# Out-projection of a flow-matching step: seven products of quarters for eight, the gate in W_out, sums joined from PSUM

## The chip, the cores and the metric

The kernel runs on one core of a Trainium2 chip. Its time is in device microseconds, the median of several runs. TensorE (PE; its weight loads are shown as PEld), VectorE (DVE), ScalarE (ACT) and GpSimd (POOL) compute; SyncE (SP) and GpSimd also issue transfers. Each engine has its own instruction queue and takes it in order; semaphores join the queues.

## The reference

One layer for two groups of tokens, 2048 sample tokens and 128 prompt tokens, model width 1024. Cut to what the change touches (the mixer's three branches, all ahead of `merged`, stay as they are):

```python
gt = jax.nn.sigmoid(gates.reshape(B, T, N_BRANCH, D_MODEL))
merged = jnp.einsum('btnd,btnd->btd', gt, pb)
out = jnp.einsum('btd,de->bte', merged, w_out)     # 1024 x 1024, the same for both groups
h = h + gate[:, None, :] * out                     # gate: one row of 1024 for each group
y = rmsnorm(h, final_g)
```

## The kernel before

A Python function records the instructions of each engine; a scheduler with its own timeline then sets their order, within data dependences and priorities (`tc.high_priority`). `order` rows below are that result. Tokens stand in 17 tiles of 128 (0 to 15 sample, 16 prompt). A float32 operand is scaled by a power of two and split into a high and a low f16 part, and a product is three f16 matmuls for each 128 of the contraction: high x high, high x low, low x high. The scale comes from a sum of squares (`A.activation(..., AF.Square, accum_out=...)`), summed over the partitions by a matmul with ones (`scales`: tiles named `...scb` go in, one column comes out).

`xh` and `xl` hold the normalized input in f16 for the whole kernel. `merge(n, ...)` runs once for each branch (order 1, 2, 0): over 8 blocks `db` of 128 model columns, over two halves of the tokens, over token blocks of 512 (one of 128): a gate product of 24 matmuls (`xh`, `xl`), a sigmoid on ACT into `sg`, a branch product of 12 (`big`, that is `o16`), a multiplication on DVE out of PSUM, an addition on POOL into `mrow`, which goes to the DRAM tensor `mD` (`mrg`). The products take their PSUM bank from `ps_mm`, a pool of three. In the last merge (n = 0) `each` is `tail`: `out_w(db)` loads one 128-column block of W_out and splits it into `whi`, `wlo` (`wohi`, `wolo` in rows), and `gate_rows` (the generator `gates`) forms the gate rows in DRAM (`gateD`). At its last block `ahead_out` prepares the first five out tiles (`out_prep`: load from `mD`, square, scale, split into `mh`, `ml`).

The out-projection then goes tile by tile, prompt tile first, then sample tiles 8 to 15 and 0 to 7: two halves of 512 columns with 24 matmuls each (`gemm_N`), on DVE a multiplication of PSUM by `gt` (the gate row times the scales' inverses, made by POOL), on POOL the addition of the x rows `xr`, on ACT the square of the row, `rsqrt` on DVE and POOL, a scaling by `final_g` on DVE, and the store. The last tile has its end split in two halves.

Of the kernel before, what the change touches and what calls it, by code (L numbers as in the profile page):

```python
# [20 lines left out]
P = 128  # L21
# [90 lines left out]
def hybrid_flow_kernel(ctx: ExitStack, tc: tile.TileContext, x_prompt, x_sample, state_delta, c, c_ctx, ln_g, w_ada,  # L112
# [65 lines left out]
    def scales(ss, pl, tag, sb16=None):  # L178

        ps = bank(ps_x, [P, 1])  # L180
        mm(ps, ones16, widened(ss, pl, tag) if sb16 is None else sb16)
        t = sb(pl, [P, 4], tag)
        V.tensor_copy(t[:, 0:1], ps)
        h = t[:, 3:4].bitcast(I32)
        V.tensor_scalar(h, t[:, 0:1].bitcast(I32), 24, None, ALU.logical_shift_right)
        V.tensor_scalar(t[:, 1:2].bitcast(I32), h, -8388608.0, 204.0 * 8388608, ALU.mult, ALU.add)
# [1175 lines left out]
    def merge(n, first, inv, each=None, halves=HALVES, mid=None, then=None):  # L1362

        steps, sinv = iter(()), None
        for db in range(KT):
# [8 lines left out]
            for h0, hn, tbs in halves:  # L1374
                mrow = sb(big, [P, hn], "mrow", bufs=2)
                if not first:
                    SY.dma_start(mrow, mD[db][:, h0:h0 + hn])
                if each is not None and (n == 0 or db > 3):
                    next(gates, 0)
                for t0, tn in tbs:  # L1380
                    if first and db == 0:
# [18 lines left out]
                    pace.tick(tn * MT)  # L1400
                    if sinv is not None:
# [40 lines left out]


    orp = pool(ctx, "orp", 1, side="right")
    whi = sb(orp, [P, KT, D], "wohi", F16)
    wlo = sb(orp, [P, KT, D], "wolo", F16)
    winv = sb(orp, [P, KT], "winv8")

    def out_w(i):
        w = load_w(w_out[0][:, i * P:(i + 1) * P], KT, hi=whi[:, :, i * P:(i + 1) * P], lo=wlo[:, :, i * P:(i + 1) * P])  # L1450
        V.tensor_mul(winv[:, i:i + 1], w.inv, sx)

    def out_prep(t, pl, tag, hl=None):
        mt = sb(pl, [P, KT, P], tag, bufs=2)
        SY.dma_start(mt, mD[:, :, t * P:(t + 1) * P].rearrange("k p t -> p k t"))
        if hl is None:
            mh = sb(orp, [P, KT, P], "mh", F16, bufs=3)
            ml = sb(orp, [P, KT, P], "ml", F16, bufs=3)
        else:
            mh = sb(wp, [P, KT, P], "whi", F16, bufs=4)  # L1460
            ml = sb(wp, [P, KT, P], "wlo", F16, bufs=4)
        ss = sb(orp, [P, 1], "mss", bufs=2)
        with tc.high_priority():
            A.activation(ml, mt, AF.Square, accum_out=ss)
            s, inv = scales(ss, orp, "msc")
            A.activation(mh, mt, AF.Copy, scale=s)  # L1466
            V.scalar_tensor_tensor(ml, mt, s, mh, ALU.mult, ALU.subtract)
        inv8 = sb(orp, [P, KT], "inv8", bufs=6)
        V.tensor_scalar(inv8, winv, inv, None, ALU.mult)
        return mh, ml, inv8  # L1470

    pre, gp = [], []

    def half_gate(i):
        t = sb(ep, [P, 512], "st", bufs=3)
        SY.dma_start(t, gateD[1:2, i * 512:(i + 1) * 512].to_broadcast([P, 512]))
        gp.append(t)

    def ahead_out(h0):
        if h0:  # L1480
            for i, t in enumerate(order[:5]):
                pre.append(out_prep(t, *((wp, "wst") if i % 3 else (big, "mrow")), None if i < 3 else wp))
            for i in range(2):
                half_gate(i)
                scale_gate(gp[i], gp[i], pre[0][2][:, 4 * i:4 * i + 4])

    def scale_gate(out, src, inv):
        k = inv.shape[-1]
        G.tensor_tensor(out.rearrange("p (k x) -> p k x", k=k), src.rearrange("p (k x) -> p k x", k=k),
                        inv.rearrange("p (k o) -> p k o", o=1).to_broadcast([P, k, P]), ALU.mult)  # L1490

    order = [16] + list(range(8, 16)) + list(range(8))
    def tail(db):
        out_w(db)
        if db == KT - 1:
            for _ in gates:
                pass

    merge(0, False, inv_, tail, HALVES[::-1], ahead_out)
    ms_.close()  # L1500
    wo = _W()
    wo.hi, wo.lo = whi, wlo
    op = pool(ctx, "op", 2)
    gb = sb(op, [P, D], "gb", bufs=1)
    SY.dma_start(gb, gateD[0:1, :].to_broadcast([P, D]))
    fg = sb(op, [P, D], "fg", bufs=1)
    SY.dma_start(fg, final_g[None, :].to_broadcast([P, D]))

    part = sb(op, [P, 2], "part", bufs=1)
    for i_, t in enumerate(order):  # L1510
        mh, ml, inv8 = pre[i_]
        xr = sb(op, [P, D], "xr")
        SY.dma_start(xr, xrows(t * P, P))
        hh = sb(op, [P, D], "hh")
        if i_:
            gt = sb(op, [P, D], "gt")
            scale_gate(gt, gb, inv8)
        for i in range(2):
            cs = slice(i * 512, (i + 1) * 512)
            ps = bank(ps_mm, [P, 512])  # L1520
            gemm_N(ps, mh, ml, wo, i * 512, 512)
            dst, gc = (hh[:, cs], gt[:, cs]) if i_ else (gp[i], gp[i])
            with tc.high_priority():
                V.tensor_tensor(dst, ps, gc, ALU.mult)
            (V if i_ == 16 else G).tensor_tensor(hh[:, cs], dst, xr[:, cs], ALU.add)
            if i_ == 16:
                A.activation(xr[:, cs], hh[:, cs], AF.Square, accum_out=part[:, i:i + 1])
        if i_ < 12:
            pre.append(out_prep(order[i_ + 5], op, "mt"))
        ss2 = sb(op, [P, 1], "hss")  # L1530
        if i_ == 16:
            G.tensor_tensor(ss2, part[:, 0:1], part[:, 1:2], ALU.add)
        else:
            A.activation(xr, hh, AF.Square, accum_out=ss2)
        rsqrt(ss2, ss2, 1.0 / D, 1)
        for cs in ([slice(0, 512), slice(512, D)] if i_ == 16 else [slice(0, D)]):
            V.scalar_tensor_tensor(hh[:, cs], hh[:, cs], ss2, fg[:, cs], ALU.mult, ALU.mult)
            SY.dma_start(y_sample[0, t * P:(t + 1) * P, cs] if t < 16 else y_prompt[0, :, cs], hh[:, cs])


_INS = ['x_prompt', 'x_sample', 'state_delta', 'c', 'c_ctx', 'ln_g', 'w_ada', 'b_ada', 'w_in', 'conv_w', 'a_log',
# [24 lines left out]
```

## Time and profile before

| | us |
|---|---|
| median of 3 runs (2187.1 to 2194.83) | 2187.12 |
| profiled execution | 2189.41 |
| its span, first to last instruction | 2187.6 |
| last merge, about | 1735 to 2001 |
| out-projection, first to last matmul | 2002.71 to 2179.8 |
| from there to the end of the span | 7.8 |

Of the page, the first lines give the busy time of each engine; a row of a group reads: line, engine, operation, output and inputs by name, shapes, count, then busy time, mean duration of one in ns, and the idle time of the engine just before, with what ended it. A matmul's own duration (379 ns at 512 columns) holds its pipeline; what it costs in a row of matmuls is the distance of two starts. The mean granted TensorE clock of the execution is 0.991.

### The profile page before, as it was taken

What the parts mean: (1) busy time and instruction counts of PE and PEld (TensorE: products, weight loads), DVE (VectorE), ACT (ScalarE), POOL (GpSimd) and SP (SyncE); (2) the same over time, 40 slices, a digit from 0 to 9 for tenths busy, and PEclk for the clock granted to TensorE, in tenths of its full rate; (3) what the DMA queues carried; (4) which work ended last, traced back from release to release, by engine and by line L of the source; (5) the groups of instructions that cost most, each with busy time, mean ns of one, the idle gap of its engine ahead of it and who ended that gap; (6) DMA issues with size and microseconds to landing.
All of it is one profiled execution on the core that took longest, in us unless ns stands there. A gap on an engine that the chain in (4) does not pass through costs nothing.

```text
span 2187.6 us, 42676 instructions
## 1 busy us (share of the span) xinstructions
PE 2123.6 (97%) x16234; PEld 1214.9 (56%) x16234; DVE 1320.9 (60%) x3150; ACT 1015.0 (46%) x2355; POOL 701.6 (32%) x862
## 2 busy tenths in 40 slices
PE   7999999999999998999899999999999999999998
PEld 3565444455555587878555556555554444444443
DVE  5746854469879698776665555765663544323454
ACT  3644744345566474554544445655543422222332
POOL 1421333223334324322312223344432221222543
PEclk9999999999999999999999999999999999999999
DMA  8424823167777664544655555766654544324542
GB/s 282 141 87 148 290 95 106 61 204 222 253 232 240 198 197 139 146 121 127 197 183 157 174 160 180 242 196 203 198 173 150 174 129 129 116 78 127 173 148 103
DMA packets 304727, 365.09 MB, mean 167 GB/s; under 512 B 39585, under 2 KB 215946, under 8 KB 302474
## 3 DMA queue, kind: packets, MB, share of 16 engines
q1 hardware_dynamic: 289386, 302.19, 45.4%
q0 software_dynamic: 12688, 51.27, 6.5%
q10 hardware_dynamic: 2448, 8.91, 1.0%
q8 instruction: 127, 2.08, 0.4%
q14 instruction: 78, 0.64, 0.1%
HBM read 234.67 MB, written 127.62 MB: 166 GB/s over the span
## 4 chain that ended last, share of the span: by engine, by line
PE 50%; DMA 4%; DVE 4%; ACT 1%; issue 1%; POOL 0%; SPq 0%; DVEq 0%; POOLq 0%; ACTq 0%
PE b L161 50%; DMA st<-br 1%; DMA ES<-ei 1%; DMA mrg<-mrow 1%; DMA wst<-in_w_in_dram 0%; DVE XB L797 0%; DVE E L798 0%; DVE big L1360 0%; DMA mrow<-mrg 0%; DMA S<-in_state_delta_dram 0%; DMA wst<-in_w_branch_dram 0%; PE b L1057 0%; ACT big L1359 0%; DMA sq__2210_18514<-qT 0%; DMA qk<-n 0%
## 5 line engine op out<-in xcount | busy, mean ns | idle before, releaser
L161 PE MATMUL b<-xh,whi 128*128 128x512 f16 (+1 forms) x1920 | 652.6, 349 | 1.4 <-DVE mrow L1395 1.0
L161 PE MATMUL b<-xl,whi 128*128 128x512 f16 (+1 forms) x1920 | 652.9, 349 | 0.0
L161 PE MATMUL b<-xh,wlo 128*128 128x512 f16 (+1 forms) x1920 | 651.6, 348 | 0.0
L161 PEld LDWEIGHTS <-whi 128*128 128x128 f16 x3904 | 358.1, 98 | 329.2 <-issue 10.2
L161 PEld LDWEIGHTS <-wlo 128*128 128x128 f16 x1952 | 191.6, 98 | 179.0 <-issue 3.6
L161 PE MATMUL b<-big,bhi 128*128 128x512 f16 (+1 forms) x960 | 249.7, 347 | 1.4 <-ACT big L1359 1.1
L1399 POOL TENSOR_TENSOR mrow<-mrow,sg 128x512 f32<-128x512 f32 (+1 forms) x80 | 92.6, 1158 | 282.9 <-DVE sg L1398 220.5
L161 PE MATMUL b<-big,blo 128*128 128x512 f16 (+1 forms) x480 | 163.1, 347 | 0.0
L1389 ACT ACTIVATE sg<-b,winv 128x512 f32<-128x512 f32 (+1 forms) x120 | 74.2, 618 | 172.0 <-PE b L161 171.1
L161 PEld LDWEIGHTS <-xh 128*128 128x128 f16 x1496 | 117.7, 98 | 28.0
L161 PEld LDWEIGHTS <-bhi 128*128 128x128 f16 x960 | 86.9, 98 | 75.6
L1398 DVE SCALAR_TENSOR_TENSOR sg<-b,binv,sg 128x512 f32<-128x512 f32 (+1 forms) x80 | 53.4, 667 | 121.4 <-PE b L161 118.7
L646 POOL TENSOR_TENSOR cy<-cy,raw 128x545 f32<-128x545 f32 (+1 forms) x48 | 66.4, 1408 | 185.7 <-ACT raw L645 185.7
L175 DVE CAST wscb<-wss 128x1 bf16<-128x1 f32 x93 | 14.3, 154 | 154.5 <-ACT wlo L209 71.4
L866 POOL COPY T<-ES 32x256 f16<-32x256 f16 x68 | 31.0, 456 | 220.1 <-DMA ES<-ei 217.6
L161 PE MATMUL b<-whi,xh 128*128 128x128 f16 x544 | 94.0, 220 | 0.0
L161 PE MATMUL b<-wlo,xh 128*128 128x128 f16 x544 | 93.9, 220 | 0.0
L161 PE MATMUL b<-whi,xl 128*128 128x128 f16 x544 | 93.8, 220 | 0.0
L161 PE MATMUL b<-wohi,mh 128*128 128x512 f16 x240 | 90.9, 379 | 1.3 <-ACT mh L1466 1.3
L161 PE MATMUL b<-wohi,ml 128*128 128x512 f16 x240 | 90.8, 379 | 0.3 <-DVE mscb L175 0.3
L161 PE MATMUL b<-wolo,mh 128*128 128x512 f16 x240 | 90.9, 379 | 0.0
L209 ACT ACTIVATE wlo<-wst 128x1024 f16<-128x1024 f32 x52 | 54.9, 1056 | 77.4 <-DMA wst<-in_w_in_dram 75.5
(456 smaller groups left out, 4298.1 us busy)
## 6 DMA issues: line engine op xcount, KB each, us to landing
wst<-in_w_in_dram SPq DMA_DIRECT2D x60, 512.0 KB
qkv<-cy POOLq DMA_DIRECT2D x12, 1089.0 KB, 5.2
st<-br SPq DMA_DIRECT2D x48, 256.0 KB
mrow<-mrg SPq DMA_DIRECT2D x18, 512.0 KB
mrow<-mrg SPq DMA_DIRECT2D x16, 576.0 KB
mrg<-mrow POOLq DMA_DIRECT2D x16, 576.0 KB, 3.6
dc<-dec SPq DMA_DIRECT2D x17, 512.0 KB
kq<-qkv SPq DMA_DIRECT2D x34, 256.0 KB
```

What stands on the lines that cost most here:

```text
L161: PE.matmul(out, l, r, start=start, stop=stop)
L175: V.tensor_copy(sb16, ss)
L209: A.activation(w.lo, st, AF.Square, accum_out=ss)
L646: G.tensor_tensor(y[:, c0:c1], y[:, c0:c1], raw[:, 1 + c0:1 + c1], ALU.mult)
L866: G.tensor_copy(T16[rows(a0, b), :, :, b], ES[0:32, :, 2 * a0 + b, :, wT])
L1389: A.activation(sg, ps, AF.Sigmoid, scale=gw.inv)
L1398: V.scalar_tensor_tensor(sg, ps, binv[:, 1:2], sg, ALU.mult, ALU.mult)
L1399: G.tensor_tensor(mr, mr, sg, ALU.add)
```

## The change

Sample tiles are taken in eight pairs. With a pair's rows as A (tile a above tile b), split at the middle of the contraction into four quarters, and W_out likewise, the four quarters of the result are built from seven products (Winograd's form) in place of eight. Of A the sums are `a21 + a22`, that minus `a11`, `a11 - a21`, and `a12` minus the second (`pair_sums`, four POOL additions); the seven operands are then split into f16 (`pair_operands`) and stand in the memory of `xl`, two pairs at a time. Of W four operands stay in `gq` and three are stored to DRAM (`tw`) and read back into the memory of `xh` when the last merge is over. The sample gate row is multiplied into W_out beforehand, so one scale for all of W_out and one for a pair (`minv`) remain, and a result is joined to the x rows in one DVE operation out of PSUM (`joined`); sums of products pass through `sg` tiles and POOL (`added`). The prompt tile comes last, with W_out without the gate, split by 128-column block as before, stored to DRAM (`uw`) and read back; its 192 matmuls have 128 columns each.

`out_weights` does the work on W_out in the last merge, one step after each token block: eight loads with a square, split, store, multiplication by the gate row and second square (`squared`, `ungated`), then eight loads again that form the quarters (`quarters`). Operations in `kept` keep their program order. `formed` takes its bank by `rot[0]`: `bank(ps_d, ...)` raises that counter once more itself, so that its parity stays.

SP's queue at the end of the last merge, before (`mrow ... 128x8x128`, `wst ... 128x8x128`, `mt` are merged rows for out tiles; `mrow ... 128x1024` belongs to the merge):

```order
L1377 DMA mrow_25225<-mrg 128x1152 [waits DMAHW5_49,DMASW3_49,Pool_49]
L1455 DMA mrow_25354<-mrg 128x8x128 [waits DMASW5_49,DMAHW6_49,DMASW4_49,Pool_49]
L1455 DMA wst_25373<-mrg 128x8x128 [waits DMAHW3_49,DVE_49]
L1455 DMA wst_25392<-mrg 128x8x128 [waits DMAHW4_49,DVE_49]
L1455 DMA mrow_25411<-mrg 128x8x128 [waits DMAHW7_49,Pool_49]
L1377 DMA mrow_25455<-mrg 128x1024 [waits DMAHW0_49,DVE_49]
L1455 DMA wst_25430<-mrg 128x8x128 [waits DMAHW1_49,DVE_49]
L1505 DMA gb_25547<-gate 128x1024 [waits DMASW6_49,DMAHW3_49,DVE_49,DMAHW4_49,PE_49,Pool_49]
```

SP's queue there, after (`xh<-tw` are the three stored quarters, `uw` prompt weights, `hh` x rows):

```order
L1377 DMA mrow_25616<-mrg 128x1024 [waits DMAHW2_49,DMASW4_49,Pool_49]
L1540 DMA wst_25590<-mrg 128x8x128 [waits DMAHW3_49,DMASW5_49]
L1540 DMA wst_25592<-mrg 128x8x128 [waits DMAHW4_49]
L1599 DMA xh_93<-tw 128x4096 [waits DMAHW6_49,DMAHW5_49,PE_49]
L1599 DMA xh_93<-tw 128x4096 [waits PE_49]
L1599 DMA xh_93<-tw 128x4096 [waits DMAHW7_49,DMAHW1_49,PE_49]
L1699 DMA whi_26852<-uw 128x1024 [waits DMAHW0_49,PE_49]
L1699 DMA wlo_26853<-uw 128x1024 [waits PE_49]
L1540 DMA mt_25719<-mrg 128x8x128 [waits DMASW6_49,DMAHW2_49,PE_49,Pool_49]
L1540 DMA mt_25721<-mrg 128x8x128 [waits DMAHW3_49]
L1605 DMA hh_25725<-in_x_sample_dram 128x1024 [waits DMAHW4_49]
L1605 DMA hh_25727<-in_x_sample_dram 128x1024 [waits DMAHW5_49]
```

Two loads of merged rows come first instead of five tiles' worth, and the second pair's (`mt`) stand behind the quarters and some prompt weights, with the x rows of the first pair behind them.

TensorE's queue at the first out matmul, before:

```order
L161 MATMUL b_25526<-big_13808,blo_25145 128x512
L161 LDWEIGHTS ones_2_89
L161 MATMUL b_25379<-mscb_25380,ones_2_89 128x1 [waits DVE_49]
L161 LDWEIGHTS mh_25356 [waits Activation_49]
L161 MATMUL b_25555<-wohi_23213,mh_25356 128x512
```

TensorE's queue between the fourth and the fifth product of the first pair, after:

```order
L161 MATMUL b_25824<-xh_93,xl_94 128x512
L161 LDWEIGHTS ones_2_89
L161 MATMUL b_25748<-mscb_25749,ones_2_89 128x1 [waits DVE_49]
L161 LDWEIGHTS xl_94 [waits DMAHW5_49]
L161 MATMUL b_25806<-xh_93,xl_94 128x512 [waits DVE_49]
```

The scale matmul of the next tile stood ahead of the first out product; that of the second pair now stands ahead of the first pair's fifth product, whose bank (`b_25806`) is the first product's.

ACT's queue in the middle of the last merge, before:

```order
L1389 ACTIVATE sg_24429<-b_24404,winv_24213 128x512 [waits PE_49,Pool_49]
L209 ACTIVATE wolo_23214,wss_24661<-wst_24659 128x8x128 [waits DMAHW5_49,Activation_49]
L209 ACTIVATE wlo_24722,wss_24723<-wst_24640 128x1024 [waits DMAHW3_49,Activation_49]
L1389 ACTIVATE sg_24475<-b_24450,winv_24213 128x512 [waits PE_49,Pool_49]
L222 ACTIVATE wohi_23213<-wst_24659,wsc_24667 128x8x128 [waits DVE_49]
```

And after:

```order
L1389 ACTIVATE sg_24247<-b_24222,winv_23952 128x512 [waits PE_49,Pool_49]
L222 ACTIVATE bhi_24099<-wst_23941,wsc_24179 128x512 [waits DVE_49]
L1480 ACTIVATE t_2970_24129,wos_23214<-ost_23969 128x1024 [waits DMAHW1_49,DVE_49,Activation_49]
L1466 ACTIVATE t_2980_24187,uss_24186<-ost_24118 128x1024 [waits DMAHW3_49,DMAHW0_49]
L209 ACTIVATE blo_24474,wss_24475<-wst_24338 128x512 [waits DMAHW4_49]
L1475 ACTIVATE t_2987_24205<-ost_24041,us_2965_24116 128x1024 [waits Activation_49]
L1389 ACTIVATE sg_24321<-b_24296,winv_23952 128x512 [waits PE_49,Pool_49]
```

Between two sigmoids there now stand a second square (L1480), a first square (L1466) and a high half (L1475), of three different blocks, each with waits of its own.

The diff, cut:

```diff
+    kept = tc.keep_in_program_order
+    def half16():
+        return sb(orp, [P, KT, P], "t16", F16, bufs=2)
+    def squared(i, st, gr):
+        ss = sb(orp, [P, 1], "uss", bufs=2)
+        kept(A.activation(half16(), st, AF.Square, accum_out=ss))
+        us_, inv = scales(ss, orp, "usc2")
...
+    def ungated(i, st, gr, us_):
+        hi, lo = half16(), half16()
+        kept(A.activation(hi, st, AF.Copy, scale=us_))
+        kept(V.scalar_tensor_tensor(lo, st, us_, hi, ALU.mult, ALU.subtract))
+        for l, t in enumerate((hi, lo)):
+            SY.dma_start(uD[i][:, l], t.rearrange("p k c -> p (k c)"))
+        kept(V.tensor_tensor(st, st, gr, ALU.mult))
+        kept(A.activation(half16(), st, AF.Square, accum_out=wos[:, i:i + 1]))
...
+    def m_scale(mts, by=None):
+        jk = half16()
+        ss = sb(orp, [P, 3], "mss", bufs=2)
+        for i, mt in enumerate(mts):
+            A.activation(jk, mt, AF.Square, accum_out=ss[:, i:i + 1])
...
+    def halved(hi, lo, src, s):
+        A.activation(hi, src, AF.Copy, scale=s)
+        V.scalar_tensor_tensor(lo, src, s, hi, ALU.mult, ALU.subtract)
+    def pair_sums(a, b):
+        s, minv = m_scale([a, b], wsc[1])
+        yield
...
+        G.tensor_tensor(sf[0][:, 0], a21, a22, ALU.add)
+        G.tensor_tensor(sf[0][:, 1], sf[0][:, 0], a11, ALU.subtract)
+        G.tensor_tensor(sf[1][:, 0], a11, a21, ALU.subtract)
+        G.tensor_tensor(sf[1][:, 1], a12, sf[0][:, 1], ALU.subtract)
...
-    merge(0, False, inv_, tail, HALVES[::-1], ahead_out)
+    merge(0, False, inv_, None, HALVES[::-1], ahead_out, work=work)
     ms_.close()
+    with tc.high_priority():
+        run(pair_operands(0, *summed[0]))
+    tw = xh.rearrange("p k t -> p (k t)")[:, 0:12288].rearrange("p (n j l k c) -> p n j l k c", n=3, j=4, l=2, k=4)
+    for n in range(3):
+        SY.dma_start(tw[:, n].rearrange("p j l k c -> p j (l k c)"), twD[:, n])
     op = pool(ctx, "op", 2)
+    loaded = [m_load(t, op, "mt") for t in PAIRS[1]]
...
+        def formed(slot, w):
+            rot[0] += 1
+            ps = bank(ps_mm if rot[0] % 2 else ps_d, [P, 512])
+            for k in range(4):
+                mm(ps, v[:, 0, slot, k, :], w[:, :, 0, k, :], k == 0, False)
+                mm(ps, v[:, 0, slot, k, :], w[:, :, 1, k, :], False, False)
+                mm(ps, v[:, 1, slot, k, :], w[:, :, 0, k, :], False, k == 3)
+            next(ahead_, 0)
+            return ps
...
+        ps = formed(0, gq[:, 0])
+        u1 = held(ps)
+        joined(ha[:, L], ps, ha[:, L])
+        u2 = joined(temp(), formed(4, gq[:, 3]), u1)
+        added(ha[:, R], u2)
+        joined(ha[:, L], formed(1, gq[:, 1]), ha[:, L])
+        ps = formed(3, tw[:, 0])
+        joined(hb[:, R], ps, hb[:, R])
+        joined(ha[:, R], ps, ha[:, R])
+        u3 = joined(temp(), formed(5, tw[:, 1]), u2)
+        added(hb[:, L], u3)
+        added(hb[:, R], u3)
+        joined(ha[:, R], formed(6, gq[:, 2]), ha[:, R])
+        final(ha, ta)
+        joined(hb[:, L], formed(2, tw[:, 2]), hb[:, L])
+        final(hb, tb)
+        run(ahead_)
...
+    for i, cs in enumerate((L, R)):
+        ps = bank(ps_mm, [P, 4, P])
+        for b_ in range(4):
...
+            gemm_N(ps[:, b_], mh, ml, wb, 0, P)
```

More of the change, by code (lines that the diff above doesn't have):

```diff
@@ L1360, in branch_block, with merge @@
             V.scalar_tensor_tensor(o16[:, 1, g, t0:t0 + tn], st, s, o16[:, 0, g, t0:t0 + tn], ALU.mult, ALU.subtract)
-    def merge(n, first, inv, each=None, halves=HALVES, mid=None, then=None):
+    def merge(n, first, inv, each=None, halves=HALVES, mid=None, then=None, work=iter(())):
         steps, sinv = iter(()), None
@@ L1444, in hybrid_flow_kernel @@
     orp = pool(ctx, "orp", 1, side="right")
[L1445 to L1470, printed above, removed]
@@ new lines, in out_weights @@
+    def out_weights():
+        for _ in gates:
+            yield
+        read, sq = None, None
+        for i in range(KT + 2):
+            was, sq = sq, squared(*read) if read is not None else None
+            read = block(i) if i < KT else None
+            if was is not None:
+                ungated(*was)
+            yield
+        order_ = [0, 4, 1, 5, 2, 6, 3, 7]
+        nxt = block(order_[0])
+        V.tensor_reduce(wos[:, KT:KT + 1], wos[:, 0:KT], AX.X, ALU.add)
+        wsc.extend(scales(wos[:, KT:KT + 1], orp, "osc"))
+        yield
+        for i in order_[1:] + [None]:
+            now, nxt = nxt, block(i) if i is not None else None
+            yield from quarters(*now)
+        for i in range(2):
+            gatec.append(sb(ep, [P, 512], "st", bufs=3))
+            SY.dma_start(gatec[i], gateD[1:2, i * 512:(i + 1) * 512].to_broadcast([P, 512]))
@@ L1479, in ahead_out, with run @@
+    def run(gen):
+        for _ in gen:
+            pass
+    summed, operands = [], []
+    PAIRS = [(t, t + 1) for t in list(range(8, 16, 2)) + list(range(0, 8, 2))]
     def ahead_out(h0):
         if h0:
[L1481 to L1485, printed above, removed]
```

187 lines of the change are left out of this document (141 added, 46 removed).

## The prediction

> **What bounds the kernel now.** I read the page's busy times first, then the stretches by window, then the chain of work in order of time around the out-projection.
>
> ```profile
> span 2187.6 us, 42676 instructions
> PE 2123.6 (97%) x16234; PEld 1214.9 (56%) x16234; DVE 1320.9 (60%) x3150; ACT 1015.0 (46%) x2355; POOL 701.6 (32%) x862
> ```
>
> TensorE is busy in 97% of the span. The last merge and the out-projection, by window (columns: length, then busy time of PE, PEld, DVE, ACT, POOL, granted clock, DMA share, GB/s):
>
> ```profile
> 1735.00:2002.00 267.00, 266.41 (x1464) 128.91 (x1462) 88.83 (x254) 69.80 (x113) 53.84 (x56) 1.00 0.36 112
> 2000.00:2050.00 50.00, 48.42 (x231) 21.87 (x230) 29.24 (x64) 18.52 (x25) 23.88 (x21) 1.00 0.57 181
> 2050.00:2100.00 50.00, 50.00 (x236) 22.70 (x235) 22.11 (x42) 14.91 (x23) 25.63 (x22) 1.00 0.44 146
> ```
>
> In both stages TensorE has no gap; the others have slack. So matmuls taken out of these stages shorten the run, as long as nothing else becomes late. The chain, and TensorE's rows at the seam:
>
> ```profile
> 1987.12 3.09 DMA mrg<-mrow
> 1992.78 7.03 DMA mrow<-mrg
> 2004.05 175.78 PE b L161 x826
> 2179.85 0.70 DVE hh L1524
> ```
> ```profile
> 1984.89 0.22 PE L161 MATMUL b<-xl,whi 128*128 128x128 f16 x1
> 1984.95 0.22 PE L161 MATMUL b<-xh,wlo 128*128 128x128 f16 x1
> 1998.43 0.38 PE L161 MATMUL b<-xh,wlo 128*128 128x512 f16 x1
> 2001.02 0.38 PE L161 MATMUL b<-big,blo 128*128 128x512 f16 x1
> 2002.71 0.39 PE L161 MATMUL b<-wohi,mh 128*128 128x512 f16 x1 [1.30 <-ACT mh L1466]
> ```
>
> The 826 matmuls are 812 of the out-projection's 816 and 14 one-column ones at some 0.03 us, so a 512-wide one takes (175.78-0.4)/812 = 0.216 us. Starts of 128-wide ones lie 0.055-0.06 us apart.
>
> **The change, part by part.**
>
> *Matmuls.* Out: 17 tiles x 48 = 816 x 0.216 = 176.2 us. In: 8 pairs x 7 products x 12 = 672 x 0.216 = 145.2, and for the prompt tile 192 of 128 columns x 0.056 = 10.7; together 155.9. Gain **20.3 us**, all of it on the path. The quarters are read in four runs of 128 elements, 1024 apart, as v4 is now:
>
> ```profile
> L161 PE MATMUL b<-wohi,mh 128*128 128x512 f16 x240 | 90.9, 379 | 1.3 <-ACT mh L1466 1.3
> L161 PE MATMUL b<-v4hi,xl 128*128 128x512 f16 x136 | 51.5, 379 | 0.0
> ```
>
> So that read costs nothing: 379 ns either way.
>
> *Work beside them.* Durations in the out-projection, 2050 to 2150, then in the last merge:
>
> ```profile
> L1525 POOL TENSOR_TENSOR hh<-hh,xr 128x512 f32<-128x512 f32 x21 | 26.6, 1266 | 56.5 <-DVE hh L1524 36.0 <-issue 20.5
> L1524 DVE TENSOR_TENSOR hh<-b,gt 128x512 f32<-128x512 f32 x20 | 13.7, 687 | 14.0 <-PE b L161 14.0
> L1537 DVE SCALAR_TENSOR_TENSOR hh<-hh,hss,fg 128x1024 f32<-128x1024 f32 x10 | 12.8, 1284 | 10.3 <-POOL hss L171 10.3
> L1534 ACT ACTIVATE xr<-hh 128x1024 f32<-128x1024 f32 x10 | 10.6, 1057 | 16.5 <-POOL hh L1525 16.5
> L1467 DVE SCALAR_TENSOR_TENSOR ml<-mt,msc,mh 128x1024 f16<-128x1024 f32 x8 | 10.3, 1285 | 1.8 <-ACT mh L1466 1.8
> L1466 ACT ACTIVATE mh<-mt,msc 128x1024 f16<-128x1024 f32 x8 | 9.2, 1149 | 28.6 <-DVE msc L186 28.6
> L171 POOL TENSOR_TENSOR hss<-hss,mhalf 128x1 f32<-128x1 f32 x10 | 5.5, 549 | 0.0
> ```
> ```profile
> L1389 ACT ACTIVATE sg<-b,winv 128x512 f32<-128x512 f32 (+1 forms) x40 | 24.7, 619 | 124.7 <-PE b L161 124.7
> L209 ACT ACTIVATE wolo<-wst 128x1024 f16<-128x1024 f32 x7 | 7.4, 1054 | 17.6 <-DMA wst<-in_w_out_dram 17.6
> ```
>
> A pair takes TensorE 84 x 0.216 = 18.1 us. DVE per pair: 8 joins from PSUM x 0.69, 2 scalings x 1.28, low halves of 3.5 x 1.285, and about 1.4 us of one-column steps: 14.0 us. ACT: 3.5 high halves x 1.15, four squares x 1.06 with 0.2 of read-out each, one copy 0.62: 9.7. POOL: four sums and three adds x 1.266, two powers x 0.55: 10.0. All fit into 18.1. But the helper that takes the banks steps its counter twice, so after the first choice the products rotate over three PSUM banks only: a bank must be emptied within the two products that follow it, 5.2 us. DVE waits in order for POOL's adds and ACT's halves at 77% load. From 0 (all hidden) to 5 us (0.6 a pair); I take **+1.0**, near the lower end, since the joins are short and POOL's sums are a pair ahead. Stores and row loads are 3 MB a pair as for two tiles now: nothing.
>
> *Last merge.* Each of eight blocks of W_out adds to ACT two squares and a high half (2 x 1.06 + 0.4 + 1.15 = 3.7 us; the old blocks had one square and one half), in program order between the sigmoids; with two f16 buffers the second square waits until the high half is stored. A store's price here is
>
> ```profile
> mrg<-mrow POOLq DMA_DIRECT2D x16, 576.0 KB, 3.6
> ACT sg L1389 <- PE b L161: 124.7, 29, 7.1
> ```
>
> of which the sigmoid and the running weight work (0.62 + 0.8) cover some: 1.5 to 2 us of waiting. That is 3.7 + 1.4 + 1.8 = 6.9 us a step, against 267/40 = 6.7 of TensorE. A sigmoid may come 7.2 us late (the two products behind it take 7.8 us until its bank is needed, less its 0.6), and ACT now waits 124.7 us for TensorE here, so a lag of 8 x 0.2 is absorbed. If each store costs 2 us more, 8 x 2.2 - 7.2 = 10 us show; a one-column matmul of each block also stands in TensorE's order without slack. 0 to 10; I take **+2.0**, near the hidden end because ACT starts with slack. The forming of quarters (some 7.7 us of DVE in four of the blocks) hides in DVE's 178 idle us of that stage. The SP loads of the merge's weights stand behind the new stores; they are issued two blocks early, so that is in the same range.
>
> *The seam.* Pair 0 needs two loads instead of five ahead of its scale. Now:
>
> ```profile
> 1990.35 0.37 SPq L1455 DMA_DIRECT2D mrow<-mrg  x1
> 1994.52 1.06 ACT L1464 ACTIVATE ml<-mrow 128x1024 f16<-128x1024 f32 x1 [2.72 <-DMA mrow<-mrg]
> 1996.33 1.06 ACT L1464 ACTIVATE ml<-wst 128x1024 f16<-128x1024 f32 x1 [0.67 <-DMA wst<-mrg]
> ```
>
> The second square ends at 1997.6, the scale matmul stands half way in the last branch product (1999.9), and the scale is ready 0.8 us later. The high half (1.15) ends at 2002.0, a second one at 2003.2; six matmuls lie in between. Products thus start as if at 2002.3 without a gap; now the 816 do at 2003.2. **-0.9** (0 to -1.5).
>
> *First stall.* From the last reader of xh (1998.65) SP issues three loads of sum quarters (3.15 MB) and 0.52 MB of prompt weights; behind them stand pair 1's merged rows (1.05 MB, which also wait for the merge's last store) and pair 0's x rows (0.52 each). The queue moves, by window:
>
> ```profile
> 1990.00:1992.00 2.00, 2.00 (x11) 0.94 (x10) 0.00 (x0) 0.69 (x1) 0.00 (x0) 1.00 0.13 26
> 1996.00:1998.00 2.00, 2.00 (x11) 0.91 (x10) 0.00 (x0) 1.15 (x2) 0.00 (x0) 1.00 1.20 291
> 10.00:20.00 10.00, 10.00 (x43) 3.76 (x42) 5.71 (x15) 0.00 (x0) 0.00 (x0) 1.00 1.08 371
> ```
>
> 291 GB/s with the merged rows' 512-byte pieces, 371 with longer ones, starting 1.8 us after the issue (1990.35 to some 1992, so 2000.5 here). The join that frees the first product's bank needs x rows: 5.24 MB, so 2014.6 to 2018.5, and 0.7 of DVE. The fifth product waits for that bank, and TensorE's queue ahead of it holds the scale matmul of pair 1, which needs both merged loads (4.72 MB) and two squares: 2015.1 to 2018.6. TensorE is there at 2002.3 + 48 x 0.216 = 2012.7. Stall 2.6 to 6.5; I take **+4.5**, the middle, as the mix is of long and short pieces.
>
> *Clock.* After TensorE's last matmul the granted clock holds for some 3 us, then falls:
>
> ```profile
> 2181.00:2183.00 2.00, 0.00 (x0) 0.00 (x0) 0.42 (x2) 0.72 (x2) 0.57 (x2) 1.00 0.00 0
> 2183.00:2185.00 2.00, 0.00 (x0) 0.00 (x0) 1.41 (x2) 0.00 (x0) 0.17 (x1) 0.74 0.09 35
> 40.00:50.00 10.00, 5.40 (x29) 4.17 (x30) 6.92 (x28) 6.33 (x13) 1.81 (x1) 0.69 0.45 159
> ```
>
> By the first two, 0.74 as a mean of 1.00 and 0.50 puts the fall near 2184, 4 us after the end; a 4.5 us stall may just reach it. The third bounds what follows a gap: 10 x 0.31 = 3.1 us. 0 to 3.1; I take **+0.5**, the stall being at the edge. The Trainium skill (TensorE: Matmul & The Clock Gate, section "HAM oscillation — how this bites in real kernels") states "no PE-idle gaps >~3.4µs"; by it the stall surely drops the clock to half, and some 3.4 us at half rate would add 1.7 us, an estimate from that page of the skill, for 2175.1. The rows above agree on a fall but put it nearer 4 us.
>
> *End.* 178 of the prompt's small matmuls (9.9 us) stand behind the last pair product and cover that pair's final scaling; the tail after the last matmul is the same split halves as now, 2187.6 - 2179.8. **0** (-0.5 to +1).
>
> Sum: -20.3 - 0.9 + 1.0 + 2.0 + 4.5 + 0.5 = **-13.2 us**. The profiled execution took 2189.41 us (span 2187.6 and 1.8 around it), 2.3 above the median 2187.12; taken off the median the forecast is **2173.9 us**.
>
> **Rivals.**
>
> *The start is covered.* The loads run at 371 GB/s and the clock holds: the stall is 2.6 or less. For it: the rows at the kernel's start; against: the short pieces behind. 2.4 us less than the sum, with no in-stage loss 2170.
>
> *The last merge becomes the bound.* ACT in lock step with its stores shows up to 10 us: 2182. For it: 6.9 us of work a step against 6.7; against: 124.7 us of ACT waiting now.
>
> *DVE and POOL take turns* (the one on the other side). Where a pair's DVE and POOL work excluded each other, a pair would take 14.0 + 10.0 = 24.0 us for 18.1: 8 x 5.9 = 47 more, 2220; it makes the change a loss beyond 21.1 us a pair (13.2 + 10.9 spread over eight). Against: 2000 to 2050 has 29.24 + 23.88 = 53.1 busy in 50 us, so they overlap at least somewhat; for it: POOL's adds sat idle 20.5 us with nothing shown that they waited for. The Trainium skill (SBUF — State Buffer, section "SBUF: two separate sides") gives a narrower lock: a vector operation with two SBUF inputs and a GpSimd one that reads SBUF exclude each other. Of the DVE work that is scalings and low halves, 7.1 us; with POOL's 10.0 it makes 17.1 of 18.1, so by that rule the pair still fits, barely.
>
> *The change does nothing:* excluded by count and the v4 row, unless the waits above eat it.
>
> **How the numbers follow.** Sum as worked out 0.53 (own range 2168 to 2180), covered start 0.15, merge as bound 0.19, turns 0.07, else 0.06. 0.5% of 2187 (10.9 us) is about what a measurement of this kernel can tell from no change: faster is below 2176.2. The first case lies there with three quarters of its chance, the second wholly: 0.40 + 0.15 + 0.04 from the rest = 0.59; slower takes the turns and a little: 0.08; same 0.33. The range 2165 to 2187 takes in the best ends (2187.1 - 20.3 - 1.5 + 2.6 - 0.5 = 2167.4, and 2 us for overlap that these bounds may miss) and the merge rival with the upper stall and clock (2182 + 2.0 + 2.6).
>
> **What would show it.** Right: 672 matmuls on quarters at 0.216 us; one gap of 3 to 6 us at the fifth product, released by DMA of merged or x rows; DVE near 75% busy from there to the end; no PE idle in the last merge beyond 3 us; the prompt's matmuls 0.056 apart. Wrong: gaps between all pairs with DVE or POOL as releaser, ACT releasing TensorE throughout the merge, or a clock below 1.00 after the seam.

## The result and the profile after

The changed kernel takes 2207.52 us (median of six runs, 2204.37 to 2212.35) against 2187.65 us of the kernel before, run beside it: a ratio of 1.0081 (95% interval 1.0058 to 1.0104). It is 19.9 us slower. 2173.9 was forecast.

The first lines of the page after. TensorE is busy for 13.4 us less than before (2123.6), in a span that is 20.6 us longer:

```profile
span 2208.2 us, 43079 instructions
PE 2110.2 (96%) x16275; PEld 1212.1 (55%) x16275; DVE 1404.9 (64%) x3229; ACT 1054.3 (48%) x2419; POOL 728.7 (33%) x870
```

TensorE's waits from the last merge to the end, by releaser (total us, times, longest). Before, the same stretch had none in the merge and two, 1.30 and 0.28 us, at the seam:

```profile
PE b L161 <- DVE oscb L175: 10.1, 1, 10.1
PE b L161 <- DVE hh L1658: 9.9, 6, 5.0
PE b L161 <- ACT bhi L222: 2.6, 2, 1.4
PE b L161 <- DVE mscb L175: 2.2, 1, 2.2
PE b L161 <- DVE sg L1658: 1.9, 3, 0.9
PE b L161 <- DVE wscb L175: 1.6, 1, 1.6
PE b L161 <- ACT sg L1389: 1.6, 2, 0.8
```

The largest is one one-column matmul (`oscb`, the common scale of W_out, in the merge); next come joins (`hh L1658`) in the out-projection. By window (length, busy time of PE, PEld, DVE, ACT, POOL, clock, DMA share, GB/s) the merge and the stretch behind the seam:

```profile
1735.00:2000.00 265.00, 248.43 (x1340) 118.56 (x1339) 138.82 (x323) 89.22 (x145) 58.45 (x53) 0.98 0.48 154
2050.00:2100.00 50.00, 41.33 (x183) 17.83 (x182) 43.65 (x64) 27.03 (x39) 34.90 (x26) 0.93 0.45 147
2100.00:2150.00 50.00, 48.61 (x229) 22.00 (x227) 38.04 (x63) 20.92 (x31) 23.62 (x21) 1.00 0.55 176
```

Executions of these kernels differ by up to 11 us ahead of the last merge, where the instructions are nearly the same (1724.57 to 1735.40 us at the point used here, over all runs below). So stages are compared from a fixed point, the last 128-token block of the merge before (1730.24 us in the kernel before, 1732.69 after):

| us | to the first product | first product to last matmul | from there to the end | sum |
|---|---|---|---|---|
| before | 272.5 | 177.1 | 7.8 | 457.4 |
| after | 291.4 | 175.9 | 8.2 | 475.5 |
| difference | +18.9 | -1.2 | +0.4 | +18.1 |

The other 2.5 us of the 20.6 lie ahead of that point and within that spread. Two things thus went wrong: the merge lost 19 us, and of the 20.3 us of matmuls saved the out-projection kept 1.2.

**The merge.** The rows of the last block's own scale, of what comes between and of the matmul that waits, from TensorE's, ScalarE's and VectorE's timelines:

```profile
1876.61 0.17 PE L161 MATMUL b<-usc2b,ones 128*128 128x1 bf16 x1
1877.49 1.28 DVE L1476 SCALAR_TENSOR_TENSOR t<-ost,us,t 128x1024 f16<-128x1024 f32 x1
1880.12 1.06 ACT L1480 ACTIVATE t<-ost 128x1024 f16<-128x1024 f32 x1 [0.59 <-DVE ost L1479]
1881.17 1.13 ACT L1475 ACTIVATE t<-ost,us 128x1024 f16<-128x1024 f32 x1
1883.66 1.23 DVE L1479 TENSOR_TENSOR ost<-ost,ogr 128x1024 f32<-128x1024 f32 x1
1887.25 1.06 ACT L1480 ACTIVATE t<-ost 128x1024 f16<-128x1024 f32 x1 [4.94 <-DMA uw<-t]
1888.83 0.16 PE L161 MATMUL b<-oscb,ones 128*128 128x1 bf16 x1 [10.09 <-DVE oscb L175]
```

At 1876.61 TensorE does the scale of the last block, nine matmuls later, at 1878.74, it stands at the common scale. Between the two lie the end of the block before (low half, gate, second square: 1877.49 to 1881.2) and the last block whole (high half, low half, gate, second square, until 1888.3). ScalarE idles 4.94 us ahead of the last square, and the row names a store that still reads the f16 buffer; but the square's own input, the gate product, ends only at 1884.89, so the store alone holds it for 2.4 us. Nothing behind that matmul on TensorE can go ahead. The gap also halves the clock (same columns as the windows above):

```profile
1884.00:1886.00 2.00, 0.00 (x0) 0.00 (x0) 0.89 (x1) 0.00 (x0) 0.00 (x0) 0.50 1.04 347
1892.00:1894.00 2.00, 2.00 (x6) 0.71 (x5) 1.88 (x5) 1.31 (x2) 0.00 (x0) 0.55 0.21 57
1894.00:1896.00 2.00, 2.00 (x11) 0.88 (x9) 0.72 (x1) 0.32 (x1) 0.00 (x0) 1.00 0.81 235
```

It was back near 1893.8, 3.3 us after matmuls resumed in a row at 1890.5, which costs 1.6 us.

**The seam.** The stall at the fifth product came, about as large as forecast: waits of 2.2 and 1.0 us, with one of 0.9 already at the fourth product, and 1.7 us lost to half clock (0.64 and 0.50 from 2040 to 2044), 5.8 in all. On the way there (GpSimd, then SyncE's queue, then TensorE):

```profile
2024.51 2.24 POOL L1399 TENSOR_TENSOR mrow<-mrow,sg 128x512 f32<-128x512 f32 x1
2027.05 0.57 POOL L1407 DMA_DIRECT2D mrg<-mrow  x1 [0.30 <-POOL mrow L1399]
2030.66 1.00 SPq L1540 DMA_DIRECT2D mt<-mrg  x2
2038.22 0.16 PE L161 MATMUL b<-mscb,ones 128*128 128x1 bf16 x1 [2.24 <-DVE mscb L175]
2039.38 0.81 PE L161 MATMUL b<-xh,xl 128*128 128x512 f16 x3 [0.99 <-DVE hh L1658]
```

The loads of the second pair go out at 2030.66, when the last store of the merge has landed, not behind the loads of the sums.

**Behind the seam.** VectorE's groups from 2024 to 2085 (mean ns behind the busy time):

```profile
L1557 DVE SCALAR_TENSOR_TENSOR xl<-ost,msc,xl 128x1024 f16<-128x1024 f32 x8 | 13.9, 1742 | 0.0
L1658 DVE SCALAR_TENSOR_TENSOR hh<-b,minv,hh 128x512 f32<-128x512 f32 x13 | 9.5, 740 | 2.3 <-PE b L161 1.9 <-DMA hh<-in_x_sample_dram 0.4
L1619 DVE SCALAR_TENSOR_TENSOR hh<-hh,hss,fg 128x1024 f32<-128x1024 f32 x4 | 7.0, 1783 | 1.0 <-POOL hss L171 1.0
L1557 DVE SCALAR_TENSOR_TENSOR xl<-mt,msc,xl 128x512 f16<-128x512 f32 x3 | 4.1, 1378 | 0.0
L1549 DVE TENSOR_TENSOR mss<-mss 128x1 f32<-128x1 f32 x4 | 3.1, 780 | 4.6 <-ACT t L1547 4.6
```

What has two inputs in SBUF is stretched: low halves to 1742 ns for 1285, scalings to 1783 for 1284, even a one-column addition to 780. Joins, with one input in PSUM, keep their 740. Single rows show how, GpSimd's first:

```profile
2045.63 2.25 POOL L1564 TENSOR_TENSOR ost<-mt 128x512 f32<-128x512 f32 x1
2046.68 2.28 DVE L1557 SCALAR_TENSOR_TENSOR xl<-ost,msc,xl 128x1024 f16<-128x1024 f32 x1
2048.88 0.74 DVE L1557 SCALAR_TENSOR_TENSOR xl<-mt,msc,xl 128x512 f16<-128x512 f32 x1
```

The sum (1.27 alone) ends at 2047.88; the low half that began at 2046.68 ends 1.1 us after that, near its own 1.28. Each seems to wait for the other and then to take its own time.

### The profile page after: what moved, and what is told of

It reads as the page before. It is cut to its first block, busy times and chain, and to the rows that moved or that the text cites. A ratio compares the mean times of both kernels' runs of the same rounds, so it can differ in the third digit from the quotient of the medians.

```text
span 2208.2 us, 43079 instructions
## 1 busy us (share of the span) xinstructions
PE 2110.2 (96%) x16275; PEld 1212.1 (55%) x16275; DVE 1404.9 (64%) x3229; ACT 1054.3 (48%) x2419; POOL 728.7 (33%) x870
## 4 chain that ended last, share of the span: by engine, by line
PE 41%; DVE 8%; DMA 7%; ACT 3%; issue 2%; POOL 1%; SPq 0%; DVEq 0%; POOLq 0%; ACTq 0%
PE b L161 41%; DMA mt<-mrg 1%; DMA wst<-in_w_in_dram 1%; DMA st<-br 1%; DMA ES<-ei 1%; DVE xl L1557 1%; DMA wst<-in_w_branch_dram 1%; DMA mrg<-mrow 0%; DVE XB L797 0%; DVE E L798 0%; DVE hh L1658 0%; DVE sg L386 0%; DVE big L1360 0%; DMA ost<-in_w_out_dram 0%; DVE wlo L223 0%
## 5 line engine op out<-in xcount | busy, mean ns | idle before, releaser
L161 PEld LDWEIGHTS <-whi 128*128 128x128 f16 x3840 | 351.7, 98 | 323.0 <-issue 11.3
L161 PEld LDWEIGHTS <-xl 128*128 128x128 f16 x1488 | 139.4, 98 | 111.3 <-issue 21.5
L1399 POOL TENSOR_TENSOR mrow<-mrow,sg 128x512 f32<-128x512 f32 (+1 forms) x80 | 102.2, 1280 | 288.5 <-DVE sg L1398 218.9
L646 POOL TENSOR_TENSOR cy<-cy,raw 128x545 f32<-128x545 f32 (+1 forms) x48 | 74.4, 1576 | 183.6 <-ACT raw L645 183.6
L175 DVE CAST wscb<-wss 128x1 bf16<-128x1 f32 x85 | 13.1, 154 | 128.8 <-ACT wlo L209 80.8
L223 DVE SCALAR_TENSOR_TENSOR wlo<-wst,wsc,whi 128x1024 f16<-128x1024 f32 x52 | 70.6, 1363 | 28.7 <-ACT whi L222 28.6
L161 PE MATMUL b<-gq,xl 128*128 128x512 f16 x384 | 86.3, 380 | 2.5 <-DVE hh L1658 1.2
```

The lines of the kernel that those rows point to most:

```text
L161: PE.matmul(out, l, r, start=start, stop=stop)
L175: V.tensor_copy(sb16, ss)
L223: V.scalar_tensor_tensor(w.lo, st, s, w.hi, ALU.mult, ALU.subtract)
L646: G.tensor_tensor(y[:, c0:c1], y[:, c0:c1], raw[:, 1 + c0:1 + c1], ALU.mult)
```

## The experiments

All stages, each from one execution (same points as above; a kernel executed once has no ratio):

| | ratio to before, 95% | to first product | out-projection | sum |
|---|---|---|---|---|
| before | | 272.5 | 177.1 | 457.4 |
| after | 1.0081 (1.0058 to 1.0104) | 291.4 | 175.9 | 475.5 |
| six_banks | 1.0039 (1.0027 to 1.0052) | 291.3 | 169.5 | 469.0 |
| osc_later | 1.0020 (1.0011 to 1.0029) | 279.6 | 177.0 | 464.8 |
| three_t16 | 1.0064 (1.0048 to 1.0080) | 290.2 | 176.9 | 475.3 |
| seam_loads | 1.0077 (1.0060 to 1.0094) | 291.5 | 177.9 | 477.6 |
| no_sums | | 292.3 | 163.4 | 463.9 |
| own_mrow | | 292.5 | 174.0 | 474.7 |
| fills | | 291.7 | 165.7 | 465.6 |
| combined | 0.9972 (0.9956 to 0.9987) | 282.3 | 162.4 | 452.9 |
| combined_pool | 0.9965 (0.9952 to 0.9978) | 278.2 | 165.5 | 452.0 |
| late_finals | 0.9944 (0.9931 to 0.9957) | 275.9 | 162.1 | 446.4 |

**The common scale one step later.**

```diff
         nxt = block(order_[0])
+        yield
         V.tensor_reduce(wos[:, KT:KT + 1], wos[:, 0:KT], AX.X, ALU.add)
```

> The changed kernel with the common scale of W_out (its sum and the one-column matmul with ones) asked for one step of the merge later. Theory (that matmul stands 20 matmuls behind the last block's own scale in TensorE's order and waits for a dozen operations of VectorE and ScalarE): the 10.1 us of waiting and 2 us of half clock in the last merge go, about 12 us less than the changed kernel, near 2195.5. Rival of the prediction (ScalarE goes in lock step with the stores through the whole merge): under 4 us saved, the waits reappear later in the merge at sigmoids and weights.

Measured: 2195.11 us, 11.8 us less in the merge. The 20 that the text counts are instructions: nine matmuls and their weight loads. With the edit 69 matmuls stand there. The waits of this run in the merge:

```profile
PE b L161 <- DVE wsc L186: 2.0, 1, 2.0
PE b L161 <- ACT bhi L222: 1.4, 1, 1.4
PE b L161 <- ACT sg L1389: 1.0, 1, 1.0
PE b L161 <- DVE oscb L175: 0.4, 1, 0.4
```

The place of one matmul was 12 of the merge's 19 us. The theory holds; a rest of 7 stays, of which these waits are 4.8 us and the half clock behind the first of them (1925.1 to 1928.5) 1.7.

**A third f16 buffer in the merge.**

```diff
-        return sb(orp, [P, KT, P], "t16", F16, bufs=2)
+        return sb(orp, [P, KT, P], "t16", F16, bufs=3)
...
-        gr = sb(orp, [P, P], "ogr", bufs=3)
+        gr = sb(orp, [P, P], "ogr", bufs=2)
...
```

> The changed kernel with three f16 buffers for W_out's halves and squares in place of two (and two for the gate pieces ogr in place of three, to make room). Theory (the order of the one matmul is the cause, the store wait only part of its 10.1 us): the 4.9 us for which the second square of the last block waited for its store go, and up to 2 us beside, so 4 to 7 us less than the changed kernel; the wait at that matmul stays at 4 to 6 us. Rival (lock step with the stores is the whole cause): 10 to 16 us less, no wait left at that matmul.

Measured: the wait at the common scale falls from 10.1 to 7.9 us, another of 2.9 at a sigmoid appears, and the merge gains 1.2. The gain was expected too high and the wait that stays too low, since the store alone held the last square for 2.4 us and not for 4.9: ScalarE waits for no such store now, and 2.2 us went. The lock step with the stores, my rival in the prediction, is not what made the merge the bound.

**Six PSUM banks.**

```diff
+    summed, operands, turn = [], [], [0]
...
-            rot[0] += 1
-            ps = bank(ps_mm if rot[0] % 2 else ps_d, [P, 512])
+            turn[0] += 1
+            ps = bank(ps_mm if turn[0] % 2 else ps_d, [P, 512])
```

> The changed kernel with the products of the pairs taking six PSUM banks in turn in place of three, nothing else. Theory (three banks make TensorE wait whenever a join on VectorE is late): the gaps behind the seam in the changed kernel's trace (0.66 + 0.21 + 0.71 + 0.78 + 1.19 + 4.98 + 1.39 = 9.9 us and some 2 us of lower clock) nearly go; about 11 us less than the changed kernel, near 2196. Rival (VectorE is short of time after the seam, its busy time is near 100% for 40 us, so banks only put the wait off): less than 4 us saved, the waits then name operands (xl) in place of joins.

Measured: 2199.03 us, 6.4 us less in the out-projection. No join releases TensorE any more; its long waits there are now

```profile
PE b L161 <- DVE mscb L175: 5.4, 1, 5.4
PE b L161 <- ACT xl L1556: 3.9, 2, 3.4
```

the scale and the operands of a following pair. So each side had a part: the banks let a late join pass (11.8 us of waits at joins went), but what made it late was still there: the waits at a following pair's scale and operands, 2.2 us behind the first product in the changed kernel, are 8.8 here (0.5 of the second row lies ahead of that product).

**What made VectorE late.** First the sums left out, then in their place fills of the same length:

```diff
-        sf = [sb(orp, [P, 2, 4, P], "ost", bufs=3) for _ in range(2)]
+        sf = [t_.rearrange("p (n k) c -> p n k c", n=2) for t_ in (a, b)]
...
-        G.tensor_tensor(sf[0][:, 0], a21, a22, ALU.add)
...
```

> The changed kernel without GpSimd's four sums of a pair (the operands are formed from the merged rows themselves, so the sample rows come out other than the reference's; TensorE, ScalarE and VectorE have the same instructions). Theory (GpSimd's additions and VectorE's operations with two inputs in SBUF exclude each other; in the changed kernel a low half took 1742 ns in the mean from 2024 to 2085 us against 1339 later, while joins out of PSUM stayed at 740): the low halves take 1.28 to 1.4 us in that stretch and the out-projection, first product to last matmul, falls from 175.9 to 163 to 169. Rival (VectorE is late because loads and ScalarE's halves come late, in order): the waits stay, 173 to 176 us.

```diff
-        G.tensor_tensor(sf[0][:, 0], a21, a22, ALU.add)
...
+        G.tensor_tensor(sf[0][:, 0, 0, 0:1], a[:, 0, 0:1], b[:, 0, 0:1], ALU.add)
+        for h in (0, 0, 1, 1, 1):
+            G.memset(sf[h], 1.0)
```

> The changed kernel with each pair's four sums on GpSimd replaced by one one-column addition of the two merged tiles (so that GpSimd waits for the same loads) and five fills of a 128x1024 tile (0.96 us each in the changed kernel's trace, 4.8 in all for the sums' 5.1); the sample rows come out other than the reference's. GpSimd is as busy and as late as with the sums, but reads nothing beside VectorE. Theory (the two engines exclude each other where both read SBUF): the low halves take 1.28 us, the out-projection falls as without the sums, 163 to 167 us from first product to last matmul. Rival (GpSimd's queue is late, and VectorE waits for the powers behind the sums): 172 to 176, as in the changed kernel.

Measured: 163.4 and 165.7 us for the out-projection, for 175.9. The groups of the run with fills, over the 61 us behind its first product:

```profile
L1566 POOL MEMSET ost<- 128x1024 f32 x24 | 22.5, 949 | 7.6 <-DVE xl L1557 6.9
L1564 POOL TENSOR_TENSOR ost<-mt,mt 128x1 f32<-128x1 f32 x5 | 1.9, 385 | 12.1 <-DMA mt<-mrg 12.1
L1557 DVE SCALAR_TENSOR_TENSOR xl<-ost,msc,xl 128x1024 f16<-128x1024 f32 x9 | 12.4, 1384 | 0.0
L1618 DVE SCALAR_TENSOR_TENSOR hh<-hh,hss,fg 128x1024 f32<-128x1024 f32 x4 | 5.1, 1284 | 1.8 <-POOL hss L171 1.8
L1557 DVE SCALAR_TENSOR_TENSOR xl<-mt,msc,xl 128x512 f16<-128x512 f32 x3 | 2.2, 743 | 0.0
L1549 DVE TENSOR_TENSOR mss<-mss 128x1 f32<-128x1 f32 x5 | 0.8, 151 | 4.8 <-ACT t L1547 4.8
```

GpSimd is nearly as busy as with the sums (36.9 us of these 61 for 40.0 from 2024 to 2085) and waits as long for its loads (12.1 us ahead of the one-column addition for 12.6), yet scalings are back at 1284, short low halves at 743, one-column additions at 151. The 1384 of the low halves is one of 2290 ns beside the last addition of the merge; the other eight took 1270 to 1280. So it is not GpSimd's queue that holds VectorE up, but its reading of SBUF: 10 to 12 us. The Trainium skill (SBUF — State Buffer, section "SBUF: two separate sides") states just this, an exclusive lock between a vector operation with two SBUF inputs and a GpSimd operation that reads SBUF; the runs agree, joins out of PSUM and fills included. Part of the 10 to 12 us is clock: matmuls at half clock cost the out-projection 3.6 us in the changed kernel, 2.9 with fills and nothing without the sums. Net of that the two runs agree on 9 to 10 us.

**The seam.** Loads first, then memory:

```diff
-    for n in range(3):
-        SY.dma_start(tw[:, n].rearrange("p j l k c -> p j (l k c)"), twD[:, n])
     op = pool(ctx, "op", 2)
-    loaded = [m_load(t, op, "mt") for t in PAIRS[1]]
...
+    rows0 = [rows_of(t) for t in PAIRS[0]]
+    loaded = [m_load(t, op, "mt") for t in PAIRS[1]]
+    for n in range(3):
+        SY.dma_start(tw[:, n].rearrange("p j l k c -> p j (l k c)"), twD[:, n])
...
```

> The changed kernel with the x rows of the first pair and the merged rows of the second issued ahead of the three loads of W_out's sums. Theory (the gap at the fifth product is these loads' place in the queue, and the gaps of the next pairs are VectorE and GpSimd catching up on it): the waits of 2.2 and 1.0 us at the fifth product and its 1.7 us of half clock go (5 us), the gaps of pairs 1 to 3 shrink by a half (5 us): 5 to 11 us less than the changed kernel. Rival (the loads are one queue, so the fourth product now waits for W_out's sums in place of them): within 3 us of the changed kernel, the first gap at the fourth product, released by DMA of tw.

Measured: no gain (1.0077), though not for the rival's reason. The scheduler kept the loads of the sums ahead; the x rows took over the wait of the merged rows and went out 6.6 us after the first product (2016.04 in this run), once the last store had landed:

```profile
2022.65 0.81 SPq L1602 DMA_DIRECT2D hh<-in_x_sample_dram  x2
2023.51 1.06 SPq L1540 DMA_DIRECT2D mt<-mrg  x2
```

So this run tells nothing of the queue. It suggests that whichever tile comes first in that pool lies over `mrow`, which the next run tests.

```diff
+    mrp = pool(ctx, "mrp", 1)
     ms_ = ExitStack()
...
-                mrow = sb(big, [P, hn], "mrow", bufs=2)
+                mrow = sb(mrp, [P, hn], "mrow", bufs=2)
...
-    fg = sb(op, [P, D], "fg", bufs=1)
+    fg = sb(mrp, [P, D], "mrow", bufs=2)
```

> The changed kernel with the merge's rows (mrow) in a pool of their own, so that the second pair's merged rows and the first pair's x rows no longer land in memory that the last store of the merge still reads; final_g takes a buffer of that pool. Theory (these loads wait for that store to land, 2030.5 us in the changed kernel, 7 us behind the last branch product): they are issued 5 to 7 us earlier, the waits at the fifth product (2.2 and 1.0 us, and 1.7 of half clock) go; first product to last matmul 175.9 becomes 167 to 172. Rival (the queue's three loads of W_out's sums ahead of them set it): 174 to 176, the same two waits.

Measured, with the first product at 2021.24:

```profile
2020.75 1.84 SPq L1541 DMA_DIRECT2D mt<-mrg  x2
PE b L161 <- DVE hh L1659: 9.6, 5, 5.0
PE b L161 <- DVE msc L186: 1.2, 1, 1.2
```

The loads go out 0.5 us ahead of the first product where it was 6.6 behind, the half clock at the seam is gone (1.00 from 2034 to 2046), and one wait of 1.2 and one of 0.9 remain of 4.1. The cause of the first stall is shown. But the out-projection gains 1.9 us only: TensorE still waits 9.6 us for joins, now all behind the seam, 2.6 of it at once at 2056.66, and behind that wait the clock is at half from 2059.6 to 2063.0. What is saved at the seam is given back where VectorE and GpSimd exclude each other.

**Together.** `combined` joins the three edits (banks, scale, `mrow`) and loads every third pair into the buffers `wst`; `combined_pool` also issues the stores of W_out's parts from GpSimd.

```diff
-            nx = [m_load(t, op, "mt") for t in PAIRS[i_ + 2]] if i_ + 2 < len(PAIRS) else None
+            nx = [m_load(t, wp if i_ % 3 == 1 else op, "wst" if i_ % 3 == 1 else "mt") for t in PAIRS[i_ + 2]] if i_ + 2 < len(PAIRS) else None
...
```

> Six banks, the common scale one step later, the merge's rows in their own pool, and every third pair's merged rows loaded into the two buffers wst that the first pair used (six buffers in place of four). If the four causes add: 10 to 12 us of the merge's 19, and 12 to 15 of the out-projection's 20 come back; 22 to 27 us less than the changed kernel, so 2 to 7 us under the kernel before. Rival (VectorE and GpSimd excluding each other is the bound behind the seam, whatever the banks and loads): 16 to 19 less, at or above the kernel before.

> As combined, and the stores of W_out's halves and of its sums issued by GpSimd in place of SyncE. Theory (in the last merge the weight loads stand in SyncE's queue behind stores that wait for VectorE, which made the waits of 2 to 3 us and the half clock that the run with the later scale still showed near 1922): 2 to 5 us less than combined. Rival (GpSimd then waits in order, its additions into mrow come late, and with them the stores of the merge): the same or up to 5 us more than combined.

Measured: 2183.11 and 2183.35 us beside 2190.72 of the kernel before, both faster than it, by 0.3%. By the sums of the stages the three edits gave 6.5, 10.7 and 0.8 us alone, 18.0 together, and `combined` gives 22.6; whether the rest is the loads into `wst`, which were never run alone, or the spread of single executions stays open. With GpSimd's stores this execution has the merge 4 us shorter and the out-projection 3 us longer; the ratios don't part the two.

```diff
+        while pending:
+            final(*pending.pop(0))
...
-        final(ha, ta)
...
+            pending.extend([(ha, ta), (hb, tb)])
...
```

> As combined_pool, and the final norm of a pair (its power on GpSimd and its scaling on VectorE) asked for after the second product of the next pair. Theory (the one long wait left in combined_pool's out-projection, 3.64 us for a join, stood behind the final scalings, which waited for powers behind GpSimd's sums): it goes with its half clock, 3 to 5 us less than combined_pool, near 0.994 of the kernel before. Rival (the same work of VectorE and GpSimd only moves): within 2 us of combined_pool.

Measured: 2181.94 us, ratio 0.9944, and the wait of 3.6 us is still there. The scheduler, which orders by its own timeline, put out the same order of instructions on every engine as for `combined_pool`: this is that program a second time. So nothing is learned of the finals, but something of the table: one program, executed twice, differs by 2.3 us to the first product, by 3.4 in the out-projection and by 5.6 in the sum. The one execution has half clock for 3.4 us in the merge and 6.8 in the out-projection, the other none and 3.4, and a wait of 1.5 us for a scale is in the first alone. Differences of a few us between two rows of the table therefore show nothing by themselves: the gains of 1.2 and 1.9 above rest on the waits that went, and the 3 us more in the out-projection of `combined_pool` are not the stores' doing, as 162.1 here shows. The two ratios, 0.9965 and 0.9944 with intervals that meet at about 0.9955 only, say that an interval of one session is somewhat too narrow; the program is 0.3 to 0.6% faster than the kernel before.

```profile
PE b L161 <- DVE hh L1661: 3.6, 1, 3.6
PE b L161 <- DVE wsc L186: 1.7, 1, 1.7
PE b L161 <- ACT bhi L222: 1.4, 1, 1.4
```

These are its long waits from the last merge to the end.

## Why the prediction was wrong

Point by point, by the terms of its sum:

- *Matmuls, -20.3: right.* 672 matmuls on quarters, at 380 ns each and 0.216 us apart where nothing waits, and 192 small ones. Their time is what the run with the sums left out comes near to (163.4, seam stall included).
- *Last merge, +2.0 in 0 to 10: this step failed.* With the seam's gain taken in, the stage lost 18.9, where 1.1 was forecast. The step counted ScalarE's work against a step of TensorE, and named in half a sentence that a one-column matmul of each block stands in TensorE's order without slack. The blocks' own matmuls indeed cost nothing. The one that I did not look up was the common scale: nine matmuls (2 us) behind the last block's own, with 12 us of serial work between them. That was 10.1 us of waiting and 1.6 of clock; taken away, 11.8 us came back. The rival "the last merge becomes the bound" had the place and up to 10 us of loss there, but not the mechanism nor the size: more buffers gave 1.2. The rest is 7.1 us in `osc_later` and 9.8 in `combined`; with the stores on GpSimd's queue it is 5.7 and 3.4 in two executions, so the stores probably had a part. What is left are waits for weights and sigmoids that no run takes apart.
- *In-stage work, +1.0 in 0 to 5: this step failed too.* What was not matmuls, first stall or its clock came to +13.3. The step compared 14.0 us of VectorE with 18.1 of TensorE, by durations from a stretch (2050 to 2150 before) in which not one scaling or low half ran beside a GpSimd addition. Without the sums 12.5 us came back, with fills 10.2. The row that could have warned is the scaling in the kernel before, 1614 ns in the mean of three at 2000 to 2050 where the quoted group had 1284:

```profile
L1537 DVE SCALAR_TENSOR_TENSOR hh<-hh,hss,fg 128x1024 f32<-128x1024 f32 x3 | 4.8, 1614 | 0.9 <-POOL hss L171 0.9
```

One of the three took 2.28 us, beside a GpSimd addition of 1.26, the other two 1.28. The rival "DVE and POOL take turns" was nearer than its 0.07: the lock is the narrow one that the prediction weighed beside it and let pass because 17.1 us fit into 18.1. That holds for an even flow, and from 2100 on there was one wait of 1.4 us. Behind the seam, the low halves of three pairs fell into the 43 us from 2041 to 2084, in which TensorE could have done 2.4 pairs at 18.1; VectorE was busy for 39.8 of them, and with three banks each late join stopped TensorE. The prediction also left the one-column operations out of the lock.
- *First stall, +4.5, and clock, +0.5: the sizes within their ranges* (3.2 at the fifth product and 0.9 at the fourth, 4.1 in all; the clock 1.7, three times the term), *the cause wrong*, so that the size of the stall agrees is luck. The loads waited for memory that the last store was reading, not for their place in the queue; the prediction named that store in brackets only.
- *Seam, -0.9, and end, 0: about right.* The first product waited 0.53 us where the kernel before waited 1.30; the end took 0.4 us more.

The sum -13.2 thus missed by 17.8 us in the merge with the seam (18.9 for 1.1), by 13.1 in the out-projection (-1.2 for -14.3) and by 0.4 at the end; another 2.5 of the profiled execution lie ahead of these stages.

## What to carry to other kernels

Where a scheduler fixes the order of an engine, look up every small operation on the bounding engine that gathers results of a long chain, and count the work between its last input and its place: one one-column matmul cost more than half of what the new algorithm saved. Count VectorE's operations with two SBUF inputs and GpSimd's readings as one resource, in the busiest 50 us and not in the mean, and take their prices from a stretch where both run. A load into memory of a closed pool waits for the last transfer out of it, whatever the queue.

## What the runs showed of the hardware

Two things I had not expected. The exclusion of the two engines reaches one-column operations: an addition of two single columns took 780 ns in the mean beside GpSimd's sums and 151 beside fills. And at the seam the half clock came although TensorE had already resumed: the last product before the gap ended at 2035.99, matmuls went on at 2039.38, and the clock fell near 2040.6, to return by 2044. The prediction put the fall near 4 us after the end of work. It came 4.6 us after it here and 4.8 in the merge, but only 1.9 us after it in the wait of 5.0 us that began at 2079.6. These three stretches of half clock in the changed kernel lasted 10.2, 3.4 and 6.8 us; matmuls ran in 3.3 to 3.8 us of each, so the price was 1.6 to 1.9 us each time. The Trainium skill's rule (TensorE: Matmul & The Clock Gate, section "HAM oscillation — how this bites in real kernels") of "no PE-idle gaps >~3.4µs" agrees with the seam's gap, 3.4 us with a single one-column matmul in it. Other gaps of these runs do not keep to it: the clock also fell behind a wait of 2.0 us in `combined_pool` (1921.68 to 1923.66, one of 0.5 shortly before it, half clock from 1923.9) and behind one of 2.6 us in `own_mrow` (2056.66 to 2059.27, half clock from 2059.6), and it stayed at 1.00 through 3.7 us with a single one-column matmul in `no_sums` (2031.76 to 2035.42). The measurements decide here: in this case the length of one gap does not tell whether the clock falls.
